# Down projections of both feed-forward blocks by seven block products, their block sums made beforehand

## The chip, the core and the metric

The kernel runs on one core of one Trainium2 chip. It is written in Python for the five engines of the core: TensorE (PE, matrix products), VectorE (DVE), ScalarE (ACT), GpSimd (POOL) and SyncE (SP, which here issues nearly all transfers). The metric is the device time of one execution in microseconds (us), with all inputs in DRAM at its start and the output in DRAM at its end. Times are compared as medians of repeated executions.

## What is computed

One layer of a bidirectional encoder: a feed-forward half step, a mixer (attention and a gated recurrence side by side), a second feed-forward half step, and a norm. There are 1024 tokens, the width is 1024, the feed-forward width is 2816, everything in float32.

```python
def swiglu_half_step(x, gain, w_in, w_out):
    h = rms_norm(x, gain)
    gate, up = jnp.split(h @ w_in, 2, axis=-1)
    return (jax.nn.silu(gate) * up) @ w_out

def reference(x, ...):
    x = x + 0.5 * swiglu_half_step(x, ffn1_norm[l], ffn1_w_in[l], ffn1_w_out[l])
    x = x + hybrid_mixer(x, l, mix_norm[l], w_in_mix[l], ...)
    x = x + 0.5 * swiglu_half_step(x, ffn2_norm[l], ffn2_w_in[l], ffn2_w_out[l])
    x = rms_norm(x, final_norm[l])
```

The change concerns the last product of both half steps, (silu(gate) * up) @ w_out: 1024 tokens by 2816 by 1024.

## The kernel before

**Products.** Every float32 operand of a product is split into a high part (rounded to the PE's float32 format by a cast on ACT, L103) and a low part (the rest, a subtraction on DVE, L104): `split`. A product of two operands is then three matmuls: high by high, high by low, low by high. A matmul has a 128x128 stationary block, a 128x512 moving block, and adds into one PSUM bank of 128x512. There are eight banks.

**Up projection (`ffn_up`).** The 2816 columns are 22 blocks f of 128. For each f the products with w_in run already as seven block products instead of eight, which are 84 matmuls. The sums of weight blocks that this needs, four per f, are made by GpSimd (L263 to L266, tiles s1 to s4). DVE makes the low parts of the seven weight operands of an f and combines the products out of PSUM (L329 to L355). SP fetches the weights of an f (L246) several f ahead, and stores the finished activation of an f, 128 features by 1024 tokens, to DRAM in two halves (L342, L356). The order of instructions in every engine's queue is set by a scheduler when the kernel is built, by the order in which the code is written and the dependences.

**Down projection (`ffn_down`).** Two groups g of four token tiles (128 tokens each). For a group, the loop over the 22 f loads a row block of w_out (512 KB, L417) and the group's part of the activation (256 KB, L419), splits them into three pairs of 128x512 tiles, and runs 24 matmuls (L446): four token tiles t by two halves d of the output by three. That is 2 x 22 x 24 = 1056 matmuls in each feed-forward block. The four tiles' results use all eight banks until the group ends. The last two f (`tail=2`; four in the second block) of a group are kept back, so that a tile's last products run tile by tile. Each tile's result is then added to the residual x (L475, 16 of these per block), and `done` follows: in the first block it stores x and makes the normed rows xn for the mixer, in the second it makes the final norm and stores the output.

**Into the mixer.** `rows_to_h` transposes the normed rows of a tile on the PE (tiles pt_n, L147) and splits the result into hm (L150 on ACT, L151 on DVE). The first products of the recurrence (`rec_early`, 48 matmuls, L167) need the hm of the first four token tiles, the products after them (rec_ps) all eight. In the first block, the first group's tiles are normed and stored long before the second group ends.

## Time and profile before

| what | value |
| --- | --- |
| time, median of 3 runs | 2057.21 us |
| lowest and highest of them | 2056.97 and 2058.83 us |
| span of the profiled execution | 2057.7 us |
| PE busy | 2009.0 us, 10549 matmuls |
| DVE / ACT / POOL busy | 1144.4 / 785.9 / 378.2 us |
| down projections begin | 463.00 us (first block), 1809.79 us (second block) |

The profiled execution is known by its span alone, 2057.7 us, 0.5 us over the median of the runs. In the rows of a group a line gives the source line, the engine, the operation, the tiles it writes and reads, the number of instructions, the busy time, the mean of one in ns, and the idle time of the engine before them with what ended it. In a timeline a row begins with its start and its duration in us. Matmuls are pipelined: one lasts 389 ns from start to end, while the next starts before it has ended. In a table of windows, `PEclk` is the granted clock of the PE as a share of the full one.

### The profile page before, as it was taken

The numbers are of one execution on the slowest core, as the hardware profiler recorded it, in microseconds if no ns is written. First come the engines' busy times: TensorE is split into PE (matmuls) and PEld (weight loads), VectorE is DVE, ScalarE is ACT, GpSimd is POOL, SyncE is SP. The second block draws the span as 40 slices with busy tenths as digits, with TensorE's granted clock in tenths as the row PEclk, the third lists the DMA queues.
The fourth block names the chain that finished last, engine by engine and source line by source line (L and its number), as shares of the span: only waits on it lengthen the run. The fifth ranks groups of instructions, "written<-read, shape, count | busy, mean of one in ns | idle before, by whom it ended". The sixth has DMA issues, their size and how long they took to land.

```text
span 2057.7 us, 27329 instructions
## 1 busy us (share of the span) xinstructions
PE 2009.0 (98%) x10549; PEld 1724.9 (84%) x10549; DVE 1144.4 (56%) x1955; ACT 785.9 (38%) x1307; POOL 378.2 (18%) x271
## 2 busy tenths in 40 slices
PE   6999999999999999999999999989999999999998
PEld 5788888888888889989999788878888888888886
DVE  7644554435363563688872558756545445354535
ACT  5433343324343332333333546633333333244232
POOL 1522232300000000020220323313322222100000
PEclk9999999999999999999999999999999999999999
DMA  6332232128464211131234542364323222275442
GB/s 216 105 93 67 90 98 87 42 72 288 151 221 151 74 32 52 31 91 43 73 102 135 164 154 72 102 208 123 91 81 93 77 77 62 72 263 187 144 148 77
DMA packets 208410, 232.09 MB, mean 113 GB/s; under 512 B 9476, under 2 KB 169496, under 8 KB 208280
## 3 DMA queue, kind: packets, MB, share of 16 engines
q1 hardware_dynamic: 205976, 221.95, 33.8%
q0 software_dynamic: 2304, 8.39, 1.0%
q8 instruction: 83, 1.36, 0.3%
q14 instruction: 47, 0.39, 0.1%
HBM read 175.78 MB, written 54.53 MB: 112 GB/s over the span
## 4 chain that ended last, share of the span: by engine, by line
PE 92%; DVE 4%; ACT 1%; DMA 1%; issue 1%; POOL 0%; SPq 0%; DVEq 0%; POOLq 0%; ACTq 0%
PE py_ffn L446 23%; PE pa_ffn L302 16%; PE pd_ffn L302 11%; PE rec_ps L167 6%; PE pc_ffn L302 5%; PE pb_ffn L302 5%; PE pp_ffn L286 3%; PE lv L632 2%; PE pa L926 2%; PE ri_ps L543 2%; PE aq_ps L543 2%; PE rg_ps L543 2%; PE py L926 2%; PE pv L901 2%; PE s L869 2%; PE ptp L888 1%
## 5 line engine op out<-in xcount | busy, mean ns | idle before, releaser
L446 PE MATMUL py_ffn<-hl_out_ffn,hl_act_ffn 128*128 128x512 f32 x1872 | 427.2, 389 | 0.0
L446 PEld LDWEIGHTS py_ffn<-hl_out_ffn,hl_act_ffn 128*128 128x128 f32 x1872 | 351.1, 188 | 72.5
L302 PE MATMUL pa_ffn<-ffn_T,hl_in_ffn_S 128*128 128x512 f32 x984 | 242.7, 389 | 0.0
L302 PE MATMUL pd_ffn<-ffn_B,hl_in_ffn_S 128*128 128x512 f32 x960 | 232.0, 389 | 0.6 <-DVE ffn_B L186 0.6
L302 PEld LDWEIGHTS pa_ffn<-ffn_T,hl_in_ffn_S 128*128 128x128 f32 x984 | 184.7, 188 | 38.3
L302 PEld LDWEIGHTS pd_ffn<-ffn_B,hl_in_ffn_S 128*128 128x128 f32 x960 | 180.1, 188 | 38.7 <-DVE ffn_B L186 1.4
L104 DVE TENSOR_TENSOR hl_out_ffn<-raw_out_ffn,hl_out_ffn 128x512 fp32r<-128x512 f32 x156 | 106.3, 689 | 187.0 <-ACT hl_out_ffn L103 186.7
L103 ACT CAST hl_in_ffn_S<-s_ffn 128x512 fp32r<-128x512 f32 x164 | 101.9, 622 | 221.4 <-PE pd_ffn L302 174.6
L104 DVE TENSOR_TENSOR hl_in_ffn_S<-s_ffn,hl_in_ffn_S 128x512 fp32r<-128x512 f32 x164 | 150.1, 918 | 65.0 <-ACT hl_in_ffn_S L103 64.8
L104 DVE TENSOR_TENSOR hl_in_ffn_A<-raw_in_ffn,hl_in_ffn_A 128x512 fp32r<-128x512 f32 x135 | 100.2, 746 | 134.3 <-ACT hl_in_ffn_A L103 134.3
L103 ACT CAST hl_out_ffn<-raw_out_ffn 128x512 fp32r<-128x512 f32 x156 | 95.3, 619 | 208.0 <-PE py_ffn L446 193.8
L103 ACT CAST hl_in_ffn_A<-raw_in_ffn 128x512 fp32r<-128x512 f32 x135 | 83.4, 624 | 162.2 <-PE pc_ffn L302 77.1
L167 PE MATMUL rec_ps<-hm,hl_rec_w 128*128 128x512 f32 x528 | 123.2, 394 | 2.3 <-DVE hm L151 2.3
L302 PE MATMUL pa_ffn<-ffn_B,hl_in_ffn_A 128*128 128x512 f32 x492 | 120.0, 390 | 1.1 <-DVE ffn_B L186 1.1
L167 PEld LDWEIGHTS rec_ps<-hm,hl_rec_w 128*128 128x128 f32 x528 | 99.8, 190 | 23.0 <-DVE hm L151 2.5
L302 PE MATMUL pc_ffn<-ffn_T,hl_in_ffn_A 128*128 128x512 f32 x492 | 118.4, 389 | 0.0
L302 PE MATMUL pb_ffn<-ffn_B,hl_in_ffn_A 128*128 128x512 f32 x492 | 118.2, 389 | 0.0
L302 PEld LDWEIGHTS pa_ffn<-ffn_B,hl_in_ffn_A 128*128 128x128 f32 x492 | 92.0, 188 | 20.9 <-DVE ffn_B L186 1.9
L302 PEld LDWEIGHTS pb_ffn<-ffn_B,hl_in_ffn_A 128*128 128x128 f32 x492 | 92.4, 188 | 19.2
L302 PEld LDWEIGHTS pc_ffn<-ffn_T,hl_in_ffn_A 128*128 128x128 f32 x492 | 92.2, 188 | 19.1
L264 POOL TENSOR_TENSOR s_ffn<-s_ffn,raw_in_ffn 128x512 f32<-128x512 f32 x41 | 65.6, 1599 | 203.2 <-issue 200.4
L263 POOL TENSOR_TENSOR s_ffn<-raw_in_ffn 128x512 f32<-128x512 f32 x41 | 54.1, 1321 | 229.0 <-DVE hl_in_ffn_S L104 224.6
(259 smaller groups left out, 3086.0 us busy)
## 6 DMA issues: line engine op xcount, KB each, us to landing
raw_in_ffn<-in_ffn_w_in SPq DMA_DIRECT2D x88, 512.0 KB, 4.1
raw_out_ffn<-in_ffn_w_out SPq DMA_DIRECT2D x88, 512.0 KB, 3.7
raw_act_ffn<-d_act SPq DMA_DIRECT2D x88, 256.0 KB, 4.0
d_act<-g_ffn SPq DMA_DIRECT2D x82, 256.0 KB, 2.2
x<-d_x SPq DMA_DIRECT2D x24, 512.0 KB, 5.1
x<-in_x SPq DMA_DIRECT2D x16, 512.0 KB, 6.5
d_x<-x SPq DMA_DIRECT2D x16, 512.0 KB, 2.8
raw_rec_w<-in_w_in_mix SPq DMA_DIRECT2D x12, 512.0 KB, 3.9
```

The costliest lines, as they stand in the source:

```text
L103: nc.scalar.copy(hl[:, 0, :], src)
L104: (lo_engine or nc.vector).tensor_sub(hl[:, 1, :], src, hl[:, 0, :].bitcast(F32))
L167: nc.tensor.matmul(out, hl[:, a, ks], h[half][b][:, k, cols], start=(k == 0 and i == 0), stop=(k == NK - 1 and i == 2),)
L263: nc.gpsimd.tensor_add(s1, a21, a22)
L264: nc.gpsimd.tensor_sub(s2, s1, a11)
L286: nc.tensor.matmul(halves(ps[j]), A[2 * j + k // 4][:, a, ks], B[k // 4][:, :, b, k % 4, lo:hi], start=(k == 0 and i == 0), stop=(k == NK ...
L302: nc.tensor.matmul(ps, A[:, a, ks], op(key)[:, b, k, :], start=(first and k == 0 and i == 0), stop=(k == 3 and i == 2), skip_group_check=True,
L446: nc.tensor.matmul(py[d], ah[:, a, o : o + P], wo[d][:, b, :], start=(f == 0 and i == 0), stop=(f == NF - 1 and i == 2),)
L543: nc.tensor.matmul(ps[:, tt, :], h[half][a][:, k, ts], hl[k // 4][:, b, ws], start=(k == 0 and i == 0), stop=(k == NK - 1 and i == 2),)
L632: nc.tensor.matmul(pl[:, cs], now[:, 0, cs], now[:, 1, cs], start=True, stop=True)
L869: nc.tensor.matmul(ps[:, ks], qT[:, a, qs], kT[:, b, kv, ks], start=(i == 0), stop=(i == 2))
L926: nc.tensor.matmul(py, lhs(a, n), units[n][:, b, ds], start=(n == 0 and i == 0), stop=(n == 3 and i == 2),)
```

## The change

Both down projections are computed by seven block products in place of eight. The activation block of a pair of f (2i and 2i+1) is cut into token halves (even and odd token tiles), w_out into halves of the output columns. With A11, A12 (even tokens; f even, f odd), A21, A22 (odd tokens) and B11, B12, B21, B22 (rows f even or odd, first or second half of the columns), there are four sums S1 to S4 of blocks of A and four sums T1 to T4 of blocks of B, and the products are A11 B11, A12 B21, S2 T2, A22 T4, S3 T3, S1 T1 and S4 B22.

- A new function `combine`, called from `ffn_up` after each f from the third on, makes the sums of a pair: for side T it loads two row blocks of w_out (512 KB each) into one tile cb, GpSimd makes the four sums in place (L377 to L380), SP stores the 1 MB tile to DRAM (L381). For side S it does so with the two activation blocks of the pair, which it reads back from DRAM (L371 to L374). There is one cb tile (`bufs=1`) for both sides. The last T and S (pair 10) come after the last f.
- `ffn_down` runs product after product, each over 11 pairs. A step loads two 128x512 blocks (256 KB each, L461), splits them as one 128x1024 tile, and runs 12 matmuls (four token tiles by three, L473): 7 x 11 x 12 = 924 matmuls per block. Products add up in banks (five sets of four, called a to e); each finished set is added to x (L500, and L539 for the last), 36 additions per block. These stand in the program after the first step of the next product.
- The odd token tiles are finished when the last product begins, and are normed, stored and transposed during it. The even tiles 0, 2, 4, 6 are finished one after the other at the very end: the last product's last pairs (`tail=3` in the first block, 7 in the second) are kept back and run tile by tile. Then come the transposes of tiles 0 and 2, `rec_early`, and the transposes of tiles 4 and 6.

Three places show how instructions are moved. The names end in numbers that differ between the builds.

GpSimd in the middle of the up projection of the first block: f = 13 and 14. Before:

```order
L263 TENSOR_TENSOR s1_ffn1_13_2403<-raw_in_ffn1_13_1_2401 128x512
L264 TENSOR_TENSOR s2_ffn1_13_2404<-s1_ffn1_13_2403,raw_in_ffn1_13_0_2399 128x512
L265 TENSOR_TENSOR s3_ffn1_13_2405<-raw_in_ffn1_13_0_2399,raw_in_ffn1_13_1_2401 128x512
L266 TENSOR_TENSOR s4_ffn1_13_2406<-raw_in_ffn1_13_0_2399,s2_ffn1_13_2404 128x512
L263 TENSOR_TENSOR s1_ffn1_14_2544<-raw_in_ffn1_14_1_2542 128x512
L264 TENSOR_TENSOR s2_ffn1_14_2545<-s1_ffn1_14_2544,raw_in_ffn1_14_0_2540 128x512
L265 TENSOR_TENSOR s3_ffn1_14_2546<-raw_in_ffn1_14_0_2540,raw_in_ffn1_14_1_2542 128x512
L266 TENSOR_TENSOR s4_ffn1_14_2547<-raw_in_ffn1_14_0_2540,s2_ffn1_14_2545 128x512
```

GpSimd at the same place with the change, where cb_T_ffn1_5 is the tile of side T, pair 5:

```order
L264 TENSOR_TENSOR s1_ffn1_13_2516<-raw_in_ffn1_13_1_2514 128x512
L265 TENSOR_TENSOR s2_ffn1_13_2517<-s1_ffn1_13_2516,raw_in_ffn1_13_0_2512 128x512
L377 TENSOR_TENSOR cb_T_ffn1_5_2504<-cb_T_ffn1_5_2504 128x512
L266 TENSOR_TENSOR s3_ffn1_13_2518<-raw_in_ffn1_13_0_2512,raw_in_ffn1_13_1_2514 128x512
L378 TENSOR_TENSOR cb_T_ffn1_5_2504<-cb_T_ffn1_5_2504 128x512
L267 TENSOR_TENSOR s4_ffn1_13_2519<-raw_in_ffn1_13_0_2512,s2_ffn1_13_2517 128x512
L379 TENSOR_TENSOR cb_T_ffn1_5_2504<-cb_T_ffn1_5_2504 128x512
L380 TENSOR_TENSOR cb_T_ffn1_5_2504<-cb_T_ffn1_5_2504 128x512
L264 TENSOR_TENSOR s1_ffn1_14_2665<-raw_in_ffn1_14_1_2663 128x512
L265 TENSOR_TENSOR s2_ffn1_14_2666<-s1_ffn1_14_2665,raw_in_ffn1_14_0_2661 128x512
L266 TENSOR_TENSOR s3_ffn1_14_2667<-raw_in_ffn1_14_0_2661,raw_in_ffn1_14_1_2663 128x512
L267 TENSOR_TENSOR s4_ffn1_14_2668<-raw_in_ffn1_14_0_2661,s2_ffn1_14_2666 128x512
```

The four sums of a pair stand between those of an f and behind those of the next, eight for GpSimd per f where there were four.

SP, the queue that issues transfers, at the end of the up projection of the first block. Before (d_act is the stored activation, raw_rec_w the mixer's weights, raw_act and raw_out operands of the down projection):

```order
L356 DMA d_act19_114<-g1_ffn1_19_3446 128x512
L342 DMA d_act20_115<-g0_ffn1_20_3464 128x512
L356 DMA d_act20_115<-g1_ffn1_20_3587 128x512
L156 DMA raw_rec_w_0_0_5450<-in_w_in_mix 128x8x128
L156 DMA raw_rec_w_0_1_5455<-in_w_in_mix 128x8x128
L156 DMA raw_rec_w_0_2_5818<-in_w_in_mix 128x8x128
L419 DMA raw_act_ffn1_3_0_3855<-d_act3_98 128x2x256
L417 DMA raw_out_ffn1_3_0_3853<-in_ffn1_w_out 128x1024
L419 DMA raw_act_ffn1_4_0_3892<-d_act4_99 128x2x256
L342 DMA d_act21_116<-g0_ffn1_21_3605 128x512
L417 DMA raw_out_ffn1_4_0_3890<-in_ffn1_w_out 128x1024
```

SP at the same place with the change (cb is the tile of sums, d_comb its copy in DRAM, raw_out_ffn1_A11_4 the operands of the first product's fifth step):

```order
L357 DMA d_act19_114<-g1_ffn1_19_3615 128x512
L368 DMA cb_S_ffn1_9_3847<-d_act19_114 128x1024
L343 DMA d_act20_115<-g0_ffn1_20_3633 128x512
L381 DMA d_combS9_126<-cb_S_ffn1_9_3847 128x2048
L368 DMA cb_T_ffn1_10_3872<-in_ffn1_w_out 128x1024 x2
L357 DMA d_act20_115<-g1_ffn1_20_3764 128x512
L381 DMA d_combT10_138<-cb_T_ffn1_10_3872 128x2048
L157 DMA raw_rec_w_0_0_5497<-in_w_in_mix 128x8x128
L157 DMA raw_rec_w_0_1_5502<-in_w_in_mix 128x8x128
L157 DMA raw_rec_w_0_2_5795<-in_w_in_mix 128x8x128
L368 DMA cb_S_ffn1_10_3880<-d_act20_115 128x1024
L461 DMA raw_out_ffn1_A11_4_4011<-d_act8_103 128x512
```

Four transfers of sums stand among the others: the store of S for pair 9, the loads and the store of T for pair 10, and the first load of S for pair 10, ahead of the operands of the fifth step.

The PE where the first block ends and the mixer begins. Before (py is the down projection's result, the first number in its name the token tile; pt_n1 the transposes of the token tile in the name):

```order
L147 MATMUL pt_n1_2_1_5559<-ident_66,xn_n1_2_4587 128x128 x4
L446 MATMUL py_ffn1_7_1_4643<-hl_out_ffn1_20_1_1_5398,hl_act_ffn1_20_1_5396 128x512
L446 MATMUL py_ffn1_7_1_4643<-hl_out_ffn1_21_1_1_5411,hl_act_ffn1_21_1_5409 128x512 x3
L147 MATMUL pt_n1_3_0_5598<-ident_66,xn_n1_3_4619 128x128 x4
L147 MATMUL pt_n1_3_1_5605<-ident_66,xn_n1_3_4619 128x128 x4
L147 MATMUL pt_n1_4_0_5612<-ident_66,xn_n1_4_5433 128x128 x4
L147 MATMUL pt_n1_4_1_5619<-ident_66,xn_n1_4_5433 128x128 x4
L167 MATMUL rec_early_0_5627<-hm_0_0_3715,hl_rec_w_0_0_5452 128x512
L167 MATMUL rec_early_1_5654<-hm_0_0_3715,hl_rec_w_0_1_5457 128x512
```

The PE at the same place with the change (pye_ffn1_3 is the last product's bank of token tile 6, pye_ffn1_2 of tile 4):

```order
L473 MATMUL pye_ffn1_2_5169<-hl_out_ffn1_S4_9_5460 128x512
L473 MATMUL pye_ffn1_2_5169<-hl_out_ffn1_S4_10_5466 128x512 x3
L473 MATMUL pye_ffn1_3_5170<-hl_out_ffn1_S4_8_5454 128x512 x3
L473 MATMUL pye_ffn1_3_5170<-hl_out_ffn1_S4_9_5460 128x512 x3
L473 MATMUL pye_ffn1_3_5170<-hl_out_ffn1_S4_10_5466 128x512 x3
L148 MATMUL pt_n1_0_0_5563<-ident_66,xn_n1_0_5480 128x128 x4
L148 MATMUL pt_n1_0_1_5570<-ident_66,xn_n1_0_5480 128x128 x4
L148 MATMUL pt_n1_2_0_5605<-ident_66,xn_n1_2_5518 128x128 x4
L148 MATMUL pt_n1_2_1_5612<-ident_66,xn_n1_2_5518 128x128 x4
L168 MATMUL rec_early_0_5620<-hm_0_0_3911,hl_rec_w_0_0_5499 128x512
```

Before, the transposes of tiles 0 to 2 stand between matmuls of the down projection, and those of tiles 3 and 4 right ahead of `rec_early`; with the change the transposes of tiles 0 and 2 stand behind the last matmul, right ahead of `rec_early`.

The diff, without the lines of the old `ffn_down`, which are printed above:

```diff
+    def ffn_up(self, name, pair, act, comb, early_lo, mid, early, loaded):
...
+        w_out = self.io[f"{name}_w_out"]
+
+        def combine(side, i):
+
+            c = self.comb.tile([P, 2, 2, 512], F32, name=f"cb_{side}_{name}_{i}", tag="cb")
+            for j in range(2):
+                f = 2 * i + j
+                src = act[f] if side == "S" else w_out[f * P : (f + 1) * P, :]
+                nc.sync.dma_start(c[:, j].rearrange("p a c -> p (a c)"), src)
+            if side == "S":
+                a11, a21, a12, a22 = (c[:, j, h] for j in range(2) for h in range(2))
+                nc.gpsimd.tensor_add(a22, a21, a22)
+                nc.gpsimd.tensor_sub(a21, a11, a21)
+                nc.gpsimd.tensor_sub(a11, a22, a11)
+                nc.gpsimd.tensor_sub(a12, a12, a11)
+            else:
+                b11, b12, b21, b22 = (c[:, j, h] for j in range(2) for h in range(2))
+                nc.gpsimd.tensor_sub(b11, b12, b11)
+                nc.gpsimd.tensor_sub(b12, b22, b12)
+                nc.gpsimd.tensor_sub(b22, b22, b11)
+                nc.gpsimd.tensor_sub(b21, b22, b21)
+            nc.sync.dma_start(comb[side][i], c.rearrange("p j h c -> p (j h c)"))
+
...
+            if f % 2 == 0:
+                combine("T", f // 2 - 1)
+            elif f > 2:
+                combine("S", (f - 3) // 2)
         next(before)
+        for side in "TS":
+            combine(side, NPAIR - 1)
+
+    def ffn_down(self, name, act, comb, load, done, follow, finish, tail):
 
...
+        lo, hi = slice(0, 512), slice(512, 1024)
+        last = NPAIR - 1
+        sources = {
+            "A11": lambda i: act[2 * i][:, lo],
+            "A12": lambda i: act[2 * i + 1][:, lo],
+            "A22": lambda i: act[2 * i + 1][:, hi],
+            "B11": lambda i: w_out[2 * i * P : (2 * i + 1) * P, lo],
+            "B21": lambda i: w_out[(2 * i + 1) * P : (2 * i + 2) * P, lo],
+            "B22": lambda i: w_out[(2 * i + 1) * P : (2 * i + 2) * P, hi],
+        }
...
+        def operands(keys, i):
...
+            raw = self.draw.tile([P, 2, 512], F32, name=f"raw_out_{nm}", tag="raw")
+            for j, key in enumerate(keys):
+                nc.sync.dma_start(raw[:, j, :], sources[key](i))
+            pool, tag = self.ab, "ab"
+            if keys[0] == "A11" and i < len(self.first):
+                pool, tag = self.first[i]
+            elif keys[0] == "S4" and i > last - tail and self.late:
+                pool, tag = self.late
+            hl = pool.tile([P, 2, 1024], F32R, name=f"hl_out_{nm}", tag=tag)
+            self.split(hl, raw.rearrange("p a c -> p (a c)"))
+            return hl
+
+        def step(hl, i, ps, j, first):
+            for n, (a, b) in enumerate(((0, 0), (0, 1), (1, 0))):
+                nc.tensor.matmul(
+                    ps, hl[:, a, j * P : (j + 1) * P], hl[:, b, hi],
+                    start=(first and i == 0 and n == 0), stop=(i == last and n == 2),
+                    skip_group_check=True,
+                )
+
...
+        def product(keys, ps, first, hooks, upto=NPAIR):
+            for i in range(upto):
+                if keys[0] == "A11" and i < len(self.first):
                     with self.tc.high_priority():
...
+                        hl = operands(keys, i)
                 else:
...
+                    hl = operands(keys, i)
+                for j in range(4):
+                    step(hl, i, ps[j], j, first)
+                for hook in hooks.get(i, ()):
+                    hook()
+
+        x = {}
+
+        def add(odd, ds, ps, sign=1.0):
+            def run():
+                for j in range(4):
+                    xt = x[2 * j + odd]
                     nc.vector.scalar_tensor_tensor(
...
+                        out=xt[:, ds], in0=ps[j], scalar=0.5 * sign, in1=xt[:, ds],
                         op0=ALU.mult, op1=ALU.add,
                     )
...
+            return run
+
+        def fetch(odd):
+            def run():
+                for j in range(4):
+                    x[2 * j + odd] = load(2 * j + odd)
+            return run
+
+        a, b = banks("pya"), banks("pyb")
+        product(("A11", "B11"), a, True, {2: [fetch(0)]})
+        product(("A12", "B21"), b, True, {0: [add(0, lo, a)]})
+        product(("S2", "T2"), a, False, {0: [add(0, lo, b)], 4: [fetch(1)]})
+        c = banks("pyc")
+        product(("A22", "T4"), c, True, {0: [add(0, hi, a)]})
+        product(("S3", "T3"), a, False, {0: [add(1, lo, c, -1.0)]})
+        d = banks("pyd")
+        product(("S1", "T1"), d, True, {0: [add(1, lo, a), add(1, hi, a)]})
+        e = banks("pye")
+        hooks = {0: [add(1, hi, d), add(0, hi, d)]}
+        for j in range(4):
+            t = 2 * j + 1
+            hooks.setdefault(1 + j, []).append(lambda t=t: done(t, x[t]))
+            hooks.setdefault(4 + j, []).append(lambda t=t: follow(t))
+        keys = ("S4", "B22")
+        split = NPAIR - tail
+        product(keys, e, True, {i: h for i, h in hooks.items() if i < split}, split)
+        ops = [(i, operands(keys, i)) for i in range(split, NPAIR)]
+        for i, h in hooks.items():
+            if i >= split:
+                for hook in h:
+                    hook()
+        for j in range(4):
+            t = 2 * j
+            for i, hl in ops:
+                step(hl, i, e[j], j, True)
+            nc.vector.scalar_tensor_tensor(
+                out=x[t][:, hi], in0=e[j], scalar=0.5, in1=x[t][:, hi], op0=ALU.mult, op1=ALU.add
+            )
+            done(t, x[t])
+            if t >= 4:
+                follow(t - 4)
+        finish()
 
 
...
+                k.comb = sbuf(up, "cb", 1)
...
-                k.draw, k.ar, k.wo, k.ah = (
-                    sbuf(down, key, n) for key, n in (("draw", 3), ("ar", 3), ("wo", 7), ("ah", 4))
-                )
+                k.draw, k.ab = sbuf(down, "draw", 4), sbuf(down, "ab", 5 if name == "ffn1" else 6)
                 if name == "ffn1":
                     k.first, k.late = ((k.wpool, "whl"), (k.fpool, "f")), None
                 else:
                     k.first = ((sbuf(down, "first", 2, side="right"), "whl"),) * 2
-                    k.late = ((sbuf(down, "late", 2 * tail, side="right"), "whl"),) * 2
+                    k.late = (sbuf(down, "late", tail, side="right"), "whl")
...
-                if t == 4:
+                if t == 0:
                     k.rec_hls = [k.rec_weights(0, j) for j in range(2)]
-                if t >= 4:
-                    k.rows_to_h(xns[t - 4], hm, t - 4, "n1", "u")
+
+            def follow1(t):
+                k.rows_to_h(xns[t], hm, t, "n1", "u")
 
             def finish1():
-                k.rows_to_h(xns[4], hm, 4, "n1", "u")
                 k.rec_early(hm)
-                for t in range(5, NT):
-                    k.rows_to_h(xns[t], hm, t, "n1", "u")
-
-            ffn(c1, "ffn1", pair1, load1, done1, dict(x=4, xn=5), opened1, nc.vector, lambda: k.vectors(k.raw), finish1, early=1)
+                for t in (4, 6):
+                    follow1(t)
+
+            ffn(c1, "ffn1", pair1, load1, done1, dict(x=8, xn=3), opened1, nc.vector, follow1, finish1,
+                lambda: k.vectors(k.raw), tail=3, early=1)
 
...
-            ffn(c4, "ffn2", pair2, load2, done2, dict(x=8, gain=1), opened2, nc.vector, tail=4)
+            ffn(c4, "ffn2", pair2, load2, done2, dict(x=8, junk=2, gain=1), opened2, nc.vector,
+                lambda t: None, lambda: None, tail=7)
```

More of the change, by code (lines that the diff above doesn't have):

```diff
@@ L28 @@
 NF = DFF // P
+NPAIR = NF // 2
 HD = 128
@@ L186, in h_op @@
         nc.vector.tensor_sub(lo, ptv, hi.bitcast(F32))
-    def ffn_up(self, name, pair, act, early_lo, mid, early, loaded):
+    def ffn_up(self, name, pair, act, comb, early_lo, mid, early, loaded):
         nc = self.nc
@@ L458, in ffn_down @@
                     with self.tc.high_priority():
-                        ops = operands(f, g)
+                        hl = operands(keys, i)
                 else:
-                    ops = operands(f, g)
-                if f == 2:
-                    for t in tiles:
-                        x[t] = load(t)
-                if f < NF - tail:
-                    for t in tiles:
-                        step(f, t, ops, py[t])
-                else:
-                    late.append((f, ops))
@@ L470, in ffn_down @@
-            for t in tiles:
-                for d in range(2):
-                    for f, ops in late:
-                        step(f, t, ops, py[t], (d,))
-                    ds = slice(d * 512, (d + 1) * 512)
+                    hl = operands(keys, i)
[8 more added lines that the diff above has]
+                    xt = x[2 * j + odd]
@@ L1071, in trunk_kernel, with ffn @@
         act = [k.scratch(f"act{f}", (P, T)) for f in range(NF)]
+        comb = {side: [k.scratch(f"comb{side}{i}", (P, 2048)) for i in range(NPAIR)] for side in "ST"}
         out, x_in = rows(io["out"]), rows(io["x"])
         keys = ("B11", "B21", "T2", "B22", "T4", "T3", "T1")
-        def ffn(ctx, name, xn_pair, load, done, d_spec, opened, early_lo, mid=None, finish=None, tail=2, early=2):
+        def ffn(ctx, name, xn_pair, load, done, d_spec, opened, early_lo, follow, finish, mid=None, tail=2, early=2):
             def sbuf(c, key, bufs, **kw):
```

61 lines of the change are left out of this document (12 added, 49 removed).

## The prediction

> **What bounds the kernel now.** I read the page first: busy times, the chain that ended last, and the costliest group.
>
> ```profile
> span 2057.7 us, 27329 instructions
> PE 2009.0 (98%) x10549; PEld 1724.9 (84%) x10549; DVE 1144.4 (56%) x1955; ACT 785.9 (38%) x1307; POOL 378.2 (18%) x271
> PE 92%; DVE 4%; ACT 1%; DMA 1%; issue 1%; POOL 0%; SPq 0%; DVEq 0%; POOLq 0%; ACTq 0%
> L446 PE MATMUL py_ffn<-hl_out_ffn,hl_act_ffn 128*128 128x512 f32 x1872 | 427.2, 389 | 0.0
> ```
>
> The PE is busy for 98% of the span and 92% of the chain runs through it; the down projections' matmuls (L446) had no idle time before them. Then the windows inside the stages, since an average of 98% need not hold in each.
>
> ```profile
> 100.00:200.00 100.00, 100.00 (x443) 82.83 (x442) 49.37 (x71) 37.49 (x65) 27.47 (x20) 1.00 0.25 76
> 500.00:600.00 100.00, 100.00 (x443) 82.83 (x442) 50.51 (x112) 38.54 (x73) 0.00 (x0) 1.00 0.57 184
> 690.00:730.00 40.00, 37.74 (x191) 31.41 (x190) 25.51 (x74) 15.94 (x35) 0.00 (x0) 0.96 0.22 79
> 1800.00:1900.00 100.00, 100.00 (x443) 82.81 (x442) 48.59 (x76) 41.05 (x72) 0.00 (x0) 1.00 0.64 219
> ```
>
> Each row gives the length of the stretch, the busy time of PE, weight loads, DVE, ACT and POOL with counts, the granted clock, the DMA share and GB/s. In the up projection (100 to 200) and in both down projections the PE is full at clock 1.00, DVE half used; only at the border to the mixer (690 to 730) does it rest. So a matmul taken out of a down projection shortens the kernel by its interval, as long as nothing else fills the place. The chain of waits gives the interval.
>
> ```profile
> 463.00 235.06 PE py_ffn L446 x1037
> 1809.79 236.65 PE py_ffn L446 x1044
> ```
>
> 235.06 / 1037 = 0.2267 us per matmul (the second row gives the same). The 389 ns of a single one are its overlapped length.
>
> **What goes.** Each down projection runs 924 matmuls where it ran 1056, so 2 x 132 = 264 go: 264 x 0.2267 = **59.8 us**. A step of 12 matmuls lasts 12 x 0.2267 = 2.72 us, an f of the up projection 84 x 0.2267 = 19.04 us.
>
> **What the down projection must keep up with.** Each step now splits one 128x1024 tile; the mixer's weights are split in that shape, and the additions have the shape of L475.
>
> ```profile
> L103 ACT CAST hl_rec_w<-raw_rec_w x12: 1045/1053/1055, 467.0 to 971.2; 128x1024 fp32r<-128x1024 f32 x12
> L104 DVE TENSOR_TENSOR hl_rec_w<-raw_rec_w,hl_rec_w x12: 1214/1223/1227, 470.3 to 975.3; 128x1024 fp32r<-128x1024 f32 x12
> L475 DVE SCALAR_TENSOR_TENSOR x<-py_ffn,x x32: 680/692/692, 573.7 to 2049.4; 128x512 f32<-128x512 f32 x32
> ```
>
> Per step ACT takes 1.05 us and DVE 1.22 us of 2.72. The 36 - 16 = 20 further additions per block take 20 x 0.69 = 13.8 us of DVE, spread over 77 steps (0.18 us each): DVE reaches 1.22 + 36 x 0.69 / 77 = 1.54 us per step. The matmuls hide all of it; uncovered, the further additions would cost 27.7 us. A step loads 512 KB, 524,288 bytes in 2.72 us = 193 GB/s. That lies below the 219 GB/s that the row for 1800 to 1900 shows with the PE full, so I cost it at nothing.
>
> **What the up projection must keep up with.** Per f GpSimd makes eight sums where it made four, and it shares something with DVE:
>
> ```profile
> 343.32 1.29 POOL L265 TENSOR_TENSOR s_ffn<-raw_in_ffn,raw_in_ffn 128x512 f32<-128x512 f32 x1 [0.63 <-DVE hl_in_ffn_S L104]
> 344.06 1.10 DVE L104 TENSOR_TENSOR hl_in_ffn_S<-s_ffn,hl_in_ffn_S 128x512 fp32r<-128x512 f32 x1 [0.83 <-ACT hl_in_ffn_S L103]
> 346.73 0.69 DVE L104 TENSOR_TENSOR hl_in_ffn_A<-raw_in_ffn,hl_in_ffn_A 128x512 fp32r<-128x512 f32 x1 [1.57 <-ACT hl_in_ffn_A L103]
> L340 DVE TENSOR_TENSOR up_ffn<-u_ffn,pc_ffn x41: 686/687/689, 82.0 to 1810.4; 128x512 f32<-128x512 f32 x41
> ```
>
> A split that begins inside a GpSimd sum takes 1.10 us, ending 0.55 us after it; the same operation alone takes 0.69. The addition with one input in PSUM (L340) never takes over 0.689 in 41 cases. So I count, as if they exclude each other, the 8 GpSimd sums at 1.29 us and the 9 DVE operations per f whose inputs both lie in SBUF (seven splits, L341 and L355) at 0.69: 8 x 1.29 + 9 x 0.69 = 16.5 us. That fits into 19.04 us, with 2.5 to spare; DVE's four operations out of PSUM (4 x 0.69 = 2.8) can run beside GpSimd. Cost: nothing, covered by the 84 matmuls; if PSUM reads were blocked too, 19.3 us would stand against 19.04.
>
> [...]
>
> SP is the other queue passed. The store of a sum (L381) waits for GpSimd, and the weight loads of later f stand behind it.
>
> ```profile
> raw_out_ffn<-in_ffn_w_out SPq DMA_DIRECT2D x88, 512.0 KB, 3.7
> raw_act_ffn<-d_act SPq DMA_DIRECT2D x88, 256.0 KB, 4.0
> d_act<-g_ffn SPq DMA_DIRECT2D x82, 256.0 KB, 2.2
> d_x<-x SPq DMA_DIRECT2D x16, 512.0 KB, 2.8
> raw_in_ffn<-in_ffn_w_in SPq DMA_DIRECT2D x88, 512.0 KB, 4.1
> ```
>
> One side of a pair takes about 4.0 (loads) + 8 GpSimd sums, its own and those between (10.3) + 2.8 (store) = 17.1 us, both sides 34.2, and a pair lasts 2 x 19.04 = 38.1 us. The single cb tile thus just suffices. I cost it at nothing, with a rival below.
>
> **What is added, place by place.**
>
> ```profile
> 17.28 0.15 DVE L83 TENSOR_SCALAR rs_n<-rs_n 128x2 int32<-128x2 int32 x1
> 17.47 1.25 DVE L84 TENSOR_SCALAR rs_n<-rs_n 128x2 int32<-128x2 int32 x1
> 1439.20 2.11 PE L302 MATMUL pa_ffn<-ffn_B,hl_in_ffn_A 128*128 128x512 f32 x8 [0.53 <-DVE ffn_B L186]
> 1441.59 0.73 PE L302 MATMUL pd_ffn<-ffn_B,hl_in_ffn_S 128*128 128x512 f32 x2 [0.28 <-DVE ffn_B L186]
> ```
>
> (1) Start of each block. There the PE waits for DVE, and four new GpSimd sums fall into it (side T first; in the second block side S, pair 0). A tiny DVE operation that met GpSimd took 1.25 us where its neighbour took 0.15. Each sum may hold DVE for up to 1.29: between 0 and 5.2 us per block. I take one in the first block (1.3) and two in the second (2.6), where two PE waits for DVE stand side by side: **+3.9**.
>
> ```profile
> 455.40 0.32 SPq L356 DMA_DIRECT2D d_act<-g_ffn  x1
> 455.00:480.00 25.00, 25.00 (x112) 20.72 (x111) 17.45 (x26) 13.52 (x23) 0.00 (x0) 1.00 0.68 234
> ```
>
> (2) First block, up to down. The store of activation 20 is issued at 455.40, that of 19 one f earlier, 436.4. Behind it in SP's order come: its landing 2.2, S of pair 9 loaded 4.0, four sums at up to 1.6 (6.4), store 2.8, T of pair 10 loaded 3.7, four sums 6.4, store 2.8, which frees cb: 464.7. Then S of pair 10 may be issued, and behind it the operands of the fifth step. The mixer's three weight loads (1.5 MB, 6.7 us at 234 GB/s) ahead keep the DMA busy until about 469; with 4.0 of landing and 2.27 of split the operands are there at 475.3. The PE wants them at 463.00 + 4 x 2.72 = 473.9. **+1.5**, between 0 and 5. In the second block these operands stand ahead of that load: 0.
>
> ```profile
> 2049.36 0.68 DVE L475 SCALAR_TENSOR_TENSOR x<-py_ffn,x 128x512 f32<-128x512 f32 x1
> 2052.93 1.42 DVE L131 SCALAR_TENSOR_TENSOR x<-x,rs_fin,g_final 128x512 f32<-128x512 f32 x2
> 698.53 0.59 ACT L150 CAST hm<-pt_n 128x512 fp32r<-128x512 f32 x1 [2.85 <-PE pt_n L147]
> 699.43 0.69 DVE L151 TENSOR_TENSOR hm<-pt_n,hm 128x512 fp32r<-128x512 f32 x1
> 706.85 11.16 PE rec_early L167 x48
> 722.87 1.65 PE L167 MATMUL rec_ps<-hm,hl_rec_w 128*128 128x512 f32 x3 [2.26 <-DVE hm L151]
> ```
>
> (3) First block into the mixer. Before, the early products follow with no gap, and the PE then rests 2.26 us. Now they need tile 2, whose last matmul ends two tiles (2 x 9 x 0.2267 = 4.1 us) ahead of the stage's end. From addition to normed rows the last tile of before took 2049.36 to 2054.35 = 5.0 us: ready 0.9 us after the end. The cast (0.59) and the subtraction (0.69) behind the transposes take 1.3 more, and DVE's share for tiles 4 and 6 (an addition each, one norm 1.5) up to 2.9: the PE rests between 2 and 5 us, I take 4.2. After them it rests about 2 as before. The clock falls: 0.96 of 40 us are 1.6 us lost at a pause of 2.26. I add 1.0 for a second pause: **+5**, from 2 to 9.
>
> [...]
>
> (4) The end. The last tile's chain is the old one, with the first half's work earlier and the stores of other even tiles beside it: **+0.5**, from -1 to 2.
>
> Sum: 3.9 + 1.5 + 5 + 0.5 = 10.9. 2057.7 - 59.8 + 10.9 = 2008.8 for a profiled execution; this one stood 0.5 above the median of the runs, so **2008.5**.
>
> **Rivals.** *All hidden:* GpSimd misses DVE at the starts, step (2) is covered, the mixer's pause takes its lower end: 2057.7 - 59.8 + 2 = about 2000. For it: the PE never waits for DVE in the stages. Against: the even tiles do end last. Chance 0.13.
>
> *SP held:* if a pair's chain takes 40 us and not 34.2 (sums at 1.6 and loads at 6 us), weight loads slip 2 us per pair, and cb never catches up: 10 pairs x 2 blocks x 2 = 40 us less the slack of loads (seven raw buffers, some 20 us per block): 0 to 40, at half 20: about 2029. Chance 0.17.
>
> *Slower, the up projection bound by DVE and GpSimd:* if GpSimd's sums lengthen each other's victims more than I count, PSUM reads included, an f takes 8 x 1.6 (like L264 below) + 13 x 0.69 = 21.8 us in place of 19.04: 2.7 x 39 f = 107 us, and 2057.7 - 59.8 + 10.9 + 107 = 2116. It decides from (59.8 - 10.9) / 39 = 1.25 us per f, that is from 20.3 us.
>
> ```profile
> L264 POOL TENSOR_TENSOR s_ffn<-s_ffn,raw_in_ffn 128x512 f32<-128x512 f32 x41 | 65.6, 1599 | 203.2 <-issue 200.4 <-POOL s_ffn L263 2.7
> ```
>
> Against it: L340's 41 cases at 0.69, and these 1.6 us hold DVE's own part, counted twice. Chance 0.06.
>
> *Nothing gained, the down projection bound by DMA:* the gain is gone at 59.8 / 154 = 0.39 us more per step, 524,288 bytes in 3.11 us = 169 GB/s; the time would be 2069 with the additions. Against: 219 GB/s were moved. Chance 0.02. That the products aren't dropped is ruled out by 924 against 1056.
>
> **How the numbers follow.** Forecast 0.62, all hidden 0.13, SP held 0.17, the slower two 0.08. With the terms' lower ends (0 + 0 + 2 - 1) the forecast case begins at 1999, with the upper ends of two of them (5 and 9) it ends near 2020; the range 1999 to 2034 takes in most of SP held. A difference of 0.2%, 4 us, is about what a measurement of this kernel can tell from no change. Faster by more: 0.91; within: 0.02; slower: 0.07.
>
> **What would show it.** Down projections of about 77 x 2.72 = 209 us each, without idle before their matmuls; the up projection's f at 19.04 us, its splits of sums longer than 0.9 us on average; GpSimd's busy time up by 176 x 1.3 = 230 us; a pause of the PE of some 4 us ahead of `rec_early`, and of under 3 at the fifth step. I am wrong if PE idle shows in the middle of an up projection, with raw_in or DVE named.

## The result, and the profile after

| | before | with the change |
| --- | --- | --- |
| median of 4 runs each | 2057.87 us | 2088.9 us |
| span of the profiled execution | 2057.7 us | 2085.6 us |

The change makes the kernel **slower**: ratio 1.0145, 95% interval 1.0132 to 1.0158. The forecast was 2008.5 us, the range 1999 to 2034.

The page of the changed kernel, its busy times and the chain that ended last:

```profile
PE 1970.4 (94%) x10285; PEld 1687.6 (81%) x10285; DVE 1297.5 (62%) x1891; ACT 793.2 (38%) x1203; POOL 658.3 (32%) x447
PE 60%; DMA 19%; POOL 10%; DVE 6%; issue 3%; ACT 2%; SPq 1%; POOLq 0%; DVEq 0%; ACTq 0%
```

The 264 matmuls are gone (10549 to 10285), and yet the span is 28 us longer. The chain no longer runs through the PE for 92% but for 60%; transfers and GpSimd hold 29% of it, where they held 1%. Whom the PE waited for, in the changed kernel (total, times, longest, in us):

```profile
PE pya_ffn L473 <- ACT hl_out_ffn_A L104: 36.5, 2, 20.9
PE pa_ffn L303 <- ACT u_ffn L334: 13.9, 4, 4.8
PE pt_ffn_T L183 <- DVE ffn_B L187: 5.3, 2, 4.7
```

The first row is the fifth step of the first product, once in each block (20.9 and 15.6 us); the second lies in the up projections; the third at the starts of the blocks. None of the three was there before. Cut at the first matmul of each stage, the two traces, that of the run without sums (first of the experiments below) and that of the fastest version compare so, in us (pp and pc are PSUM tiles: pp takes the first products of a block, pc one of the seven products of an f):

| stretch | before | change | without sums | fastest |
| --- | --- | --- | --- | --- |
| start, to the first pc matmul | 66.5 | 73.5 | 66.9 | 66.5 |
| up, to the first down matmul | 396.3 | 409.9 | 396.4 | 398.1 |
| down, to `rec_early` | 243.8 | 242.7 | 219.6 | 227.5 |
| mixer, to the first pp matmul of block 2 | 659.2 | 660.8 | 662.4 | 657.9 |
| start of block 2, to its first pc | 66.9 | 73.0 | 67.0 | 67.1 |
| up | 376.9 | 388.8 | 376.9 | 376.4 |
| down, to the end | 248.1 | 236.9 | 218.3 | 219.0 |
| span | 2057.7 | 2085.6 | 2007.5 | 2012.5 |

The change stands 78.1 us over the run without sums: 12.6 at the two starts, 25.4 in the two up projections, 41.7 in the two down projections, less 1.6 in the mixer.

**One pair's chain.** The chain of waits from one store of side T (pair 6) to the next (pair 7), start and length of each piece:

```profile
338.93 4.18 DMA d_combT<-cb_T_ffn
343.21 5.23 DMA cb_S_ffn<-d_act
348.44 6.21 issue
354.65 1.51 POOL cb_S_ffn L371
...
361.27 5.23 DMA d_combS<-cb_S_ffn
366.51 4.87 DMA cb_T_ffn<-in_ffn_w_out
371.45 1.23 POOL cb_T_ffn L377
...
380.38 4.19 DMA d_combT<-cb_T_ffn
```

There is no gap in it: store of T, load of S, sums, store of S, load of T, sums, 41.4 us, while the PE needs 38.1 us for two f. The 6.21 us marked "issue" are a further wait, which a row of DVE and SP's rows in the same window show:

```profile
335.97 1.78 DVE L356 TENSOR_TENSOR g_ffn<-g_ffn,up_ffn 128x512 f32<-128x512 f32 x1
343.64 0.40 SPq L247 DMA_DIRECT2D raw_in_ffn<-in_ffn_w_in  x1
344.08 0.93 SPq L357 DMA_DIRECT2D d_act<-g_ffn  x1
350.67 0.32 SPq L368 DMA_DIRECT2D cb_S_ffn<-d_act  x1
```

The second half of S reads an activation from DRAM. DVE had it ready at 337.75, but SP stored it only at 344.08: it stood at the store of T until 338.93, and then at the first load of S until 343.21, when the store of T had landed and the tile was free. The load goes out at 350.67, when the activation's store has landed. That landing took 6.6 us, where the median for these stores is 2.2 us in the kernel before, 2.6 in the run with the transfers alone (run 3 below) and 5.0 in the change. So one chain goes through SP, the DMA queues and GpSimd and back to SP. Over the up projection it falls behind: the stores of T for pairs 1 and 9 are these.

```profile
131.30 0.33 SPq L381 DMA_DIRECT2D d_combT<-cb_T_ffn  x1
460.22 0.33 SPq L381 DMA_DIRECT2D d_combT<-cb_T_ffn  x1
```

328.9 us for eight pairs, 41.1 each. The delay reaches the PE in two ways. In the up projection the sums of the next f stand in GpSimd's order behind a sum of a pair whose operand has not landed (L265 behind L377 below); ACT's cast waits for GpSimd, and everything on ACT stands behind the cast (GpSimd's rows, ACT's, then the PE's, at the second of these stalls; in brackets the idle time before and what ended it):

```profile
412.42 1.28 POOL L377 TENSOR_TENSOR cb_T_ffn<-cb_T_ffn 128x512 f32<-128x512 f32 x1 [7.69 <-DMA cb_T_ffn<-in_ffn_w_out]
413.65 1.30 POOL L265 TENSOR_TENSOR s_ffn<-s_ffn,raw_in_ffn 128x512 f32<-128x512 f32 x1
414.99 0.62 ACT L104 CAST hl_in_ffn_S<-s_ffn 128x512 fp32r<-128x512 f32 x1 [12.45 <-POOL s_ffn L265]
420.20 0.57 ACT L334 COPY u_ffn<-pa_ffn 128x512 f32<-128x512 f32 x1
420.82 5.49 PE L303 MATMUL pa_ffn<-ffn_T,hl_in_ffn_S 128*128 128x512 f32 x12 [3.60 <-ACT u_ffn L334]
```

GpSimd idled 7.69 us for the load, ACT 12.45 us for a GpSimd sum, and ACT copied the PE's bank only then. The twelve matmuls behind the pause take 5.3 us until the next group starts, 2.7 at full clock (the granted clock is 0.68 from 420 to 430 us). And at the end of the up projection the chain is not finished:

```profile
476.25 0.33 SPq L368 DMA_DIRECT2D cb_S_ffn<-d_act  x1
487.13 0.32 SPq L381 DMA_DIRECT2D d_combS<-cb_S_ffn  x1
500.44 0.33 SPq L381 DMA_DIRECT2D d_combT<-cb_T_ffn  x1
500.82 4.71 SPq L157 DMA_DIRECT2D raw_rec_w<-in_w_in_mix  x3
507.42 0.43 SPq L461 DMA_DIRECT2D raw_out_ffn_A<-d_act  x1
515.28 20.82 PE L473 MATMUL pya_ffn<-hl_out_ffn_A 128*128 128x512 f32 x84 [20.88 <-ACT hl_out_ffn_A L104]
```

S of pair 9, T of pair 10 and the mixer's weights go out first, then the fifth step's operands at 507.42; the PE, through with four steps, idles 20.88 us.

### The profile page after: what moved, and what is told of

Same layout as the page of the kernel before. It is cut to its first block, busy times and chain, and to the rows that moved or that the text cites. A ratio compares the mean times of both kernels' runs of the same rounds, so it can differ in the third digit from the quotient of the medians.

```text
span 2085.6 us, 27167 instructions
## 1 busy us (share of the span) xinstructions
PE 1970.4 (94%) x10285; PEld 1687.6 (81%) x10285; DVE 1297.5 (62%) x1891; ACT 793.2 (38%) x1203; POOL 658.3 (32%) x447
## 4 chain that ended last, share of the span: by engine, by line
PE 60%; DMA 19%; POOL 10%; DVE 6%; issue 3%; ACT 2%; SPq 1%; POOLq 0%; DVEq 0%; ACTq 0%
PE pya_ffn L473 7%; PE rec_ps L168 6%; PE pa_ffn L303 5%; DMA d_act<-g_ffn 3%; DMA cb_T_ffn<-in_ffn_w_out 3%; DMA d_combS<-cb_S_ffn 3%; PE pd_ffn L303 3%; DMA cb_S_ffn<-d_act 3%; PE pye_ffn L473 3%; PE pyd_ffn L473 3%; PE pyc_ffn L473 3%; PE pp_ffn L287 3%; PE lv L696 2%; PE pa L990 2%; PE ri_ps L607 2%
## 5 line engine op out<-in xcount | busy, mean ns | idle before, releaser
L303 PE MATMUL pa_ffn<-ffn_T,hl_in_ffn_S 128*128 128x512 f32 x984 | 250.1, 398 | 13.9 <-ACT u_ffn L334 13.9
L303 PEld LDWEIGHTS pa_ffn<-ffn_T,hl_in_ffn_S 128*128 128x128 f32 x984 | 189.1, 193 | 55.2 <-ACT u_ffn L334 15.6
L105 DVE TENSOR_TENSOR hl_in_ffn_S<-s_ffn,hl_in_ffn_S 128x512 fp32r<-128x512 f32 x164 | 183.9, 1134 | 60.8 <-ACT hl_in_ffn_S L104 60.4
L105 DVE TENSOR_TENSOR hl_in_ffn_A<-raw_in_ffn,hl_in_ffn_A 128x512 fp32r<-128x512 f32 x135 | 148.3, 1102 | 72.8 <-ACT hl_in_ffn_A L104 72.6
L105 DVE TENSOR_TENSOR hl_out_ffn_S<-raw_out_ffn_S,hl_out_ffn_S 128x1024 fp32r<-128x1024 f32 x88 | 106.6, 1221 | 70.0 <-ACT hl_out_ffn_S L104 69.4
L105 DVE TENSOR_TENSOR hl_out_ffn_A<-raw_out_ffn_A,hl_out_ffn_A 128x1024 fp32r<-128x1024 f32 x66 | 89.3, 1364 | 83.5 <-ACT hl_out_ffn_A L104 82.8
L104 ACT CAST hl_out_ffn_S<-raw_out_ffn_S 128x1024 fp32r<-128x1024 f32 x88 | 92.4, 1053 | 113.8 <-PE pya_ffn L473 32.0
L473 PE MATMUL pya_ffn<-hl_out_ffn_S 128*128 128x512 f32 x528 | 120.3, 389 | 0.0
L473 PEld LDWEIGHTS pya_ffn<-hl_out_ffn_S 128*128 128x128 f32 x528 | 99.1, 188 | 20.6
L104 ACT CAST hl_out_ffn_A<-raw_out_ffn_A 128x1024 fp32r<-128x1024 f32 x66 | 69.0, 1052 | 120.6 <-DMA raw_out_ffn_A<-in_ffn_w_out 68.7
```

Of the source, the lines that this page charges most:

```text
L104: nc.scalar.copy(hl[:, 0, :], src)
L105: (lo_engine or nc.vector).tensor_sub(hl[:, 1, :], src, hl[:, 0, :].bitcast(F32))
L303: nc.tensor.matmul(ps, A[:, a, ks], op(key)[:, b, k, :], start=(first and k == 0 and i == 0), stop=(k == 3 and i == 2), skip_group_check=True,
L473: nc.tensor.matmul(ps, hl[:, a, j * P : (j + 1) * P], hl[:, b, hi], start=(first and i == 0 and n == 0), stop=(i == last and n == 2), skip ...
```

## The experiments

Three theories were set against each other. **Queue**: one tile, one chain, longer than a pair. **Port** (a name only): GpSimd's eight sums per f and DVE exclude each other. **Transfers**: the added traffic slows every load. Each run stands beside runs of the kernel before on the same chip, 2058.4 to 2059.3 us. Runs 1 to 7, 9, 10 and 12 are single executions. The mixer's stretch, which none of their edits touches, takes between 656.6 and 662.4 us in them, so a few us between two of these runs mean little.

**1. No sums at all.** The calls of `combine` go, and the products read blocks that are there anyway:

```diff
-                    lambda i, side=side, j=j: comb[side][i][:, j * 512 : (j + 1) * 512]
+            sources[f"S{n}"] = lambda i, n=n: act[2 * i + n % 2][:, lo if n < 3 else hi]
...
-                combine("T", f // 2 - 1)
```

> Leaves out all block sums: no loads, no GpSimd sums and no stores of them; the down projections read unsummed blocks in their place, so all their matmuls and transfers stay. If the sums are what costs (whatever the way), the PE's two waits at the start of the down projections (20.9 and 15.6 us) and its four waits in the up projections (13.9 us) are gone, and the time is 2057 - 60 + 3 to 8 for the borders = 2000 to 2005 us. If the new down projection itself is what costs (its order of loads, its splits), the waits of 20.9 and 15.6 us stay and the time is above 2040 us.

Measured: 2009.25 us, 4 above the expected band. All of the waits named in it are gone. The new down projections themselves do what was forecast: the borders cost 2007.5 - (2057.7 - 59.8) = 9.6 us in the spans. All else that the change loses, 78 us, comes with the sums.

**2. GpSimd's sums alone, no transfers.** The tile is set to zero once and never loaded or stored:

```diff
-                nc.sync.dma_start(c[:, j].rearrange("p a c -> p (a c)"), src)
...
-            nc.sync.dma_start(comb[side][i], c.rearrange("p j h c -> p (j h c)"))
```

> GpSimd makes all its sums, but on one tile that is never loaded or stored; the down projections read unsummed blocks. Theory queue (the sums of a pair hang in one chain of load, sums and store through the single cb tile, longer than the 38.1 us of a pair, and SP and GpSimd stand still in it): the chain is gone, an f of the up projection takes 19.04 us, and the time is within 10 us of the run without sums. Theory port (GpSimd's eight sums per f and DVE exclude each other): the up projections stay about 10 to 20 us longer each, and the time is 2030 to 2060 us.

Measured: 2041.84 us, which looks like the port theory. But with nothing to wait for, the sums were moved forward: all 88 of the first block were done by 218 us, at about twice the change's rate, the first of them at the start of the program, where the PE waits for DVE:

```profile
PE pt_ffn_B L183 <- DVE x L1190: 21.2, 4, 12.3
```

The first pc matmul comes 23.1 us later than in run 1, and the two up projections are 5.4 and 5.1 us longer than there. So it showed the price of sums at another place and at another rate, and the question had to be put again, as run 5.

**3. The transfers alone, no sums.** Loads and stores stay; the eight GpSimd calls go.

> All loads and stores of the block sums stay, through the single cb tile, but GpSimd's sums on it are left out, so that copies are stored. Theory queue: a side then takes about 5 us of load and 5 us of store, 20 us for a pair instead of 41, which is under 38.1; the waits go to under 5 us in all and the time is 2003 to 2015 us. Theory transfers (the additional 4 MB per pair slow all loads and stores): time and waits stay near those of the change, above 2060 us. Theory port: like the queue theory, so this run tells nothing between those two.

Measured: 2020.41 us, 5 above the band of the queue theory and far from that of the transfers theory. The excess lies at the starts: the first pc matmul comes at 71.3 us instead of 66.9, and block 2's start takes 72.3 instead of 67.0. Its first load of T, 1 MB, stands among the first of the block.

**4. Two tiles.**

```diff
-                    for key, n in (("raw", 7), ("wop", 9), ("s", 4), ("n", 3), ("c", 4))
+                    for key, n in (("raw", 6), ("wop", 9), ("s", 4), ("n", 3), ("c", 4))
-                k.comb = sbuf(up, "cb", 1)
+                k.comb = sbuf(up, "cb", 2)
```

> Two cb tiles in place of one, and six buffers for the loaded up weights in place of seven, for room. Theory queue: the load of a side no longer waits for the store of the other, a pair's chain falls from 41 us by some 8 to 10 us to below 38.1, no lag is built up; the end of the up projection still has two sides to make (some 15 us late operands): waits of 0 to 10 us at the start of the down projections, time 2015 to 2040 us. Theory port or transfers: as the change, 2080 to 2095 us.

Measured: 2022.73 us, in the band of the queue theory, with all sums and transfers as in the change. 66 of its 78 us go with one more tile of 8 KB per partition, and its longest wait at a down projection is 4.7 us. A lag is left all the same: the stores of S for pairs 1 and 9 are issued at 154.01 and 470.34 us, 39.5 us per pair, where the change has 154.05 and 487.13, 41.6 per pair.

**5. The sums in their place, no transfers.** As run 1, with four more sums behind those of each f from the third on (160 in all, where the change has 176):

```diff
             nc.gpsimd.tensor_sub(s4, a12, s2)
+            if f >= 2:
+                for j, a in enumerate((a11, a12, a21, a22)):
+                    nc.gpsimd.tensor_sub(keep[0][:, j], a, keep[0][:, j])
```

> As the run without sums, but GpSimd makes four further sums per f right behind the four of that f, on one tile that is neither loaded nor stored: GpSimd's work of the change in its place, without the chain. It differs from the run with GpSimd's sums alone in that no sum can be made early, at the start of the block, where the PE waits for DVE. Theory queue: within 8 us of the 2009 us without sums. Theory port: the up projections are longer, 2030 to 2050 us.

Measured: 2008.21 us, 1 us from run 1, and its up projections are about 0.6 us longer each. The port theory falls for the body of the up projections at this rate of sums. It is not that the two engines leave each other alone: the group of DVE's splits of sums in the kernel before, in the change and in this run (the first row gives count, busy time in us and mean in ns; the other two count, min/median/max in ns, first and last start):

```profile
L104 DVE TENSOR_TENSOR hl_in_ffn_S<-s_ffn,hl_in_ffn_S 128x512 fp32r<-128x512 f32 x164 | 150.1, 918 | 65.0 <-ACT hl_in_ffn_S L103 64.8
L105 DVE TENSOR_TENSOR hl_in_ffn_S<-s_ffn,hl_in_ffn_S x164: 674/1096/1837, 69.1 to 1826.6; 128x512 fp32r<-128x512 f32 x164
L105 DVE TENSOR_TENSOR hl_in_ffn_S<-s_ffn,hl_in_ffn_S x164: 675/1096/1789, 62.0 to 1764.6; 128x512 fp32r<-128x512 f32 x164
```

The median split takes 1.10 us in the last two, in the slow kernel and in the fast one. The lengthened splits fit behind the 84 matmuls of an f, as the sum of 16.5 of 19.04 us had said.

**6. GpSimd issues the stores.**

```diff
-            nc.sync.dma_start(comb[side][i], c.rearrange("p j h c -> p (j h c)"))
+            nc.gpsimd.dma_start(comb[side][i], c.rearrange("p j h c -> p (j h c)"))
```

> One cb tile as in the change, but GpSimd issues the store of the sums itself, behind its last sum, so SP no longer stands still for GpSimd and the stores of the activations behind it go out in time. If SP standing still is what makes the chain too long, a pair falls from 41 us to 37 or 38, little lag is built up, and the time is 2030 to 2055 us. If the single tile alone sets the chain (load, sums, store, one side after the other), a pair stays at 40 to 41 us and the time is 2070 to 2090 us.

Measured: 2058.55 us, 30 less than the change, 3.5 above the band. Stores of T for pairs 1 and 9 are issued 317.4 us apart (133.11 and 450.49 in its timeline), 39.7 us per pair, not 37 or 38: SP's standing still is a part, 1.4 us per pair; the 1.6 us that are left over 38.1 were not parted further. The two ways come apart here: the up projections take 397.8 and 378.0 us, 1.4 and 1.0 over run 1, so nearly all of their 25.4 us is gone, while the down projections still lose 21.7 and 13.8 us and the starts 6.8 and 6.3. Its waits in the first product still come to 25.6 us.

**7. The last pair's sums during the second product.**

```diff
-        for side in "TS":
-            combine(side, NPAIR - 1)
...
         product(("A11", "B11"), a, True, {2: [fetch(0)]})
+        for side in "TS":
+            self.combine(side, NPAIR - 1)
```

> One cb tile as in the change, but the sums of the last pair are made during the second product of the down projection (in a tile of the down projection's own), so their loads and stores no longer stand ahead of the first product's operands on SP. The lag in the up projections stays (their ends 20 and 12 us late against before). If the waits of 20.9 and 15.6 us at the start of the down projections come from these transfers standing ahead, they go to under 5 us each and the time is 2089 - 36 - 4 (half clock behind the waits) = 2045 to 2060 us. If they come from the lag itself, they stay above 10 us each and the time is above 2070 us.

Measured: 2077.77 us; the expectation was missed. The waits at the first product fell from 36.5 to 10.6 us, but 7.0 new ones came at the second product, and the up projections waited a little more:

```profile
PE pa_ffn L303 <- ACT u_ffn L334: 16.7, 5, 4.8
PE pya_ffn L473 <- ACT hl_out_ffn_A L104: 10.6, 2, 6.4
PE pyb_ffn L473 <- ACT hl_out_ffn_A L104: 7.0, 3, 4.4
```

SP's row for the store of S of pair 9 stands at 490.33 us, still ahead of the fifth step's operands (496.03): the lag alone is enough to block them.

**8. Two tiles, the last pair late, T of pair 0 behind S of pair 0.** Runs 4 and 7 together, and

```diff
+            if f == 3:
+                combine("T", 0)
-            if f % 2 == 0:
+            if f % 2 == 0 and f > 2:
                 combine("T", f // 2 - 1)
```

> Two cb tiles (six up weight buffers), the last pair during the down projection, and T of pair 0 made after the start of the block, behind S of pair 0 in the code. Theory queue: no lag, no wait at the down projections, no sums among the first operations: 2009 us of the run without sums plus 0 to 8: 2009 to 2017 us. Theory port: GpSimd and DVE still exclude each other as often as in the change, 2030 us or more.

Measured: 2034.38 us (ratio 0.9878, 0.9862 to 0.9895), faster than before, but missed by 17 us, and slower than run 4. Two things show in its trace. The first pc matmul comes at 75.0 us though no sum is early: the x tiles are loaded through the buffers of the up weights, of which it has six, as run 4 has (73.4 us); with seven, in run 11, it comes at 66.5. And the late pair costs 8.1 us of waits at the second product.

**9 and 10. One side alone, one tile.** One of the two calls of `combine` goes, and the products read unsummed blocks for that side.

> Only the sums of w_out (side T) are made, through the single cb tile; the sums of the activation are left out and the products read unsummed activation blocks. Theory queue: a side takes about 20 us of a pair's 38.1, so no lag is built up and no wait over 5 us appears at the down projections; what stays is the start of the blocks (T of pair 0 among the first operations, 5 to 7 us each): 2009 + 5 to 14 = 2014 to 2023 us. A cost that grows with the amount of sums or transfers (half of them are left) would leave about half of the 78 us: 2040 to 2055 us.

> Only the sums of the activation (side S) are made, through the single cb tile; the products read unsummed blocks of w_out. Theory queue: no lag, as with side T alone, and none of the first operations of a block is a sum, since S of pair 0 needs two finished f: 2009 + 0 to 8 = 2009 to 2017 us. A cost that grows with the amount: 2040 to 2055 us.

Measured: T alone 2023.09, S alone 2006.47 us, both close to their bands of the queue theory. Neither waits at the fifth step. If the loss grew with the work, each should have kept about 39 us of it; S alone keeps none, T alone 14; its first start is 6.9 us later (first pc at 73.8 us) and its second up projection 8.6 us longer. T alone runs through its pairs 0 to 10 early, its stores issued from 23.64 to 206.92 us, 18.3 us a pair, since nothing but the tile holds it back; two such sides in one tile leave less than 2 us of 38.1.

**11 and 12. The fastest version, and the same with one tile.** Two tiles, the room from the split weights (`("raw", 7), ("wop", 8)`), T of pair 0 as in run 8, and T of the last pair already with the last f:

```diff
+            if f == NF - 1:
+                combine("T", NPAIR - 1)
...
-        for side in "TS":
-            combine(side, NPAIR - 1)
+        combine("S", NPAIR - 1)
```

> Two cb tiles, the room for the second from the split weights (eight in place of nine) and not from the loaded weights; T of pair 0 behind S of pair 0, T of the last pair already with the last f, so that only S of the last pair comes after the up projection. Theory queue: neither lag nor sums at the start; one short wait at a down projection: 2009 to 2020 us, below the 2022.7 us of two tiles with six weight buffers, whose start was held up since x is loaded through these buffers. If eight split weights are too few for the PE, waits on casts show in the up projections and the time is above 2025 us.

Measured: **2013.38 us** (5 runs, 2008.17 to 2014.38), ratio to before 0.9775, interval 0.9761 to 0.9788. It beats both kernels: 45 us under before, 75 under the change. Its starts are those of before, and one wait is left:

```profile
PE pya_ffn L476 <- ACT hl_out_ffn_A L104: 6.4, 1, 6.4
```

> The order of the fastest version (T of pair 0 behind S of pair 0, T of the last pair with the last f), but one cb tile and nine split weights as in the change: parts the second tile from the order. Theory queue: the starts of the blocks are as without sums (7 and 6 us less than in the change), but a pair still takes about 41 us through the single tile, the lag of 20 us and the waits at the down projections stay above 8 us each: 2060 to 2080 us. If the order is what brought the gain and the second tile nothing: 2010 to 2025 us.

Measured: 2081.96 us, 2 above the band. The same order with one tile has its waits back:

```profile
PE pya_ffn L476 <- ACT hl_out_ffn_A L104: 34.9, 2, 19.2
PE pa_ffn L303 <- ACT u_ffn L334: 19.6, 7, 7.5
```

The first start is repaired (first pc at 66.1 us), the lag is not: the second tile is worth 69 us in that order, while the order without it is worth 7.

## Why the prediction was wrong, point by point

- **What goes, 59.8 us.** Right. Run 1 leaves the down projections as they are in the change: block 2's takes 218.3 us where it took 248.1, 29.8 less for 132 matmuls.
- **The down projection keeps up.** Right: DMA, ACT and DVE kept pace with its steps; the rival bound by DMA did not come.
- **The up projection keeps up, GpSimd and DVE.** Right, with the caveat of run 2. The splits of sums went from 918 ns on average to 1134. The lengthening cost next to nothing in the body of the up projections, as the 16.5 us against 19.04 had said, and run 5 bears that out: with the same median of 1.10 us its up projections are about 0.6 us longer each. Why DVE's operations take longer beside GpSimd's was not shown. GpSimd's busy time rose by 280 us (378.2 to 658.3), where 230 had been forecast.
- **One side of a pair takes 17.1 us, both 34.2, "I cost it at nothing".** This is the step that failed. The chain measures 41.4 us. Against its terms: the stores took 4.3 and 5.2 us, 9.5 where 5.6 were counted, because the row that priced them was that of 512 KB and a side is 1 MB. Loads took 4.9 us for T, and for S 11.4, since its second half waits for a store of the activation that SP had held back and that itself landed slowly; 16.4 where 8.0 were counted. The sums took 6.6 and 8.9 us, 15.5 where 20.6 were counted: of the sums of f, two stood among the eight of the pair, where eight had been counted. The sum is 7.2 short, and the bound of 38.1 lay in between. A margin of 4 us on a chain of five unmeasured terms was no margin.
- **The rival SP held** was this mechanism, with about the right period (40 us). The period was partly luck: with sums at 1.6 and loads at 6 us its own terms give 2 x (6 + 12.8 + 2.8) = 43.2, and the sums were in fact shorter than counted, the stores and the load of S longer. Its price was wrong: 20 us, with the loads' slack taken off. The up projections did lose 25.4 us, but the lag came due a second time behind them: the chain's last links stood ahead of the down projections' operands, 41.7 us. That second payment was nowhere in the sum, and the slower rival was tied to the wrong engine pair.
- **(1) Starts, +3.9.** Measured 6.6 + 6.0 = 12.6 against run 1. Of this run 3, with transfers and no sums, already has 4.4 and 5.3, and run 12, where T of pair 0 is made later, has neither (66.1 and 67.0 us): most of it goes with the 2 MB of load and store that stand among the block's first transfers, and the sum had counted only GpSimd. In the first block's start SP issues the reload t1b of the first sum at 22.77 us with the change, at 22.91 in run 3 and at 19.60 without sums. How the delay reaches the PE was not tried, and an early T does not always cost as much: with T alone and with two tiles the second block's start takes 68.4 and 68.7 us.
- **(2) Up to down, +1.5 and 0.** Measured 23.1 and 18.6 us, the wait and the slow clock behind it. The 39 us from the load of S of pair 9 (476.25) to the matmul (515.28) are close to the 36.7 worked out for these links; but they begin 38 us later than assumed, as the chain lags, and as SP issues the activation store that this load needs only at 468.69.
- **(3) Into the mixer, +5.** In run 1 the first block's down projection and border cost 5.7 over the gain, and 3.2 more show up to block 2, which is within what that stretch varies between runs. The PE's pauses ahead of `rec_early` come to 2.8 us there (1.54, 0.59, 0.48 and 0.19), where 4.2 was taken. The sum is right in size, its parts were not measured one by one. **(4) The end, +0.5:** 0.1.
- **The clock.** Behind the 20.88 us pause the 84 matmuls take 20.66 us to the next group's start (515.28 to 535.94) for 19.04 at full speed, 1.6 us lost; the granted clock from 515 to 536 us is 0.92. It is 0.50 from 515.2 to 517.0, 0.56 from there to 518.7, and 1.00 from 518.7 to 525.

## What to carry to other kernels

A helper that loads, works and stores through one buffer is a chain with a period of its own: add up every link at its own size, landing included, and compare it with the period of the engine that it must keep up with; here a margin of a tenth was none. What lagged was paid twice here, since the queues worked in order, first by the instructions behind the waiting one, and again at the next stage, whose first loads stand behind the chain's last ones. Try a second buffer for such a chain first (here it took away 66 of 78 us, and issuing the stores from another engine 30), and look for its first and last links at the borders of the stage.
